# Moving the loads of the lanes earlier in a hybrid layer: the weight join, the rows of W1, the gains of W2 and W3, and the kept gate and up products

## The chip, the core and the metric

The kernel runs on one core of a Trainium2 chip. The core has five engines with a queue each: TensorE (PE) multiplies, VectorE (DVE) does elementwise arithmetic, ScalarE (ACT) does activations and copies, GpSimd (POOL) helps with elementwise work, and SyncE (SP) issues most of the transfers (DMA). ACT and POOL issue some transfers too. An engine runs its list strictly in the order in which the compiler left it, and an instruction that waits holds up all that stand behind it on its engine. Engines wait for each other by semaphores.

The metric is device time in microseconds for one execution, less is better. The kernel before took 2001.74 us (median of three runs, 1999.65 to 2007.75).

## The reference

One decoder layer over 2048 tokens of width 1024, all in fp32:

```python
hn = rms_norm(h, mix_pre_g)
proj = hn @ w_in
q = proj[..., :D_Q].reshape(B, S, N_Q_HEADS, HEAD_DIM)
k, v = ...                                   # 2 key heads
u = proj[..., D_Q + 2 * D_KV:]
attn_out = sliding_window_attention(q, k, v, attn_sinks, rel_bias)
conv_out = conformer_conv(u, conv_dw, conv_dw_b, conv_ln_g, conv_ln_b, w_conv_pw)
mixed = jnp.concatenate([attn_out, conv_out], axis=-1) @ w_out
h = h + rms_norm(mixed, mix_post_g)
hn = rms_norm(h, ffn_pre_g)
ff = (jax.nn.silu(hn @ w_gate) * (hn @ w_up)) @ w_down
h = h + rms_norm(ff, ffn_post_g)
```

The attention has a window of 128 tokens, 8 query heads on 2 key heads, a learned sink for each head and a relative bias. The convolution path is a gated unit, a causal depthwise convolution of 31 taps, a layer norm over the channels, a swish and a 512x512 product (`w_conv_pw`). The feed-forward width is 2816.

## The kernel before

**Products.** A product in fp32 is made from three products of a shorter format: each operand is split into a high part (ACT casts it: `split_w`, L133, and `split_f`, L811) and a low part (DVE or POOL subtracts: L135, L814), and PE adds high x high, high x low and low x high in PSUM (`three`, L188, `product`, L893). Rows and weights are split once and the halves kept (`lo_in`, `lo_out` hold the low halves of weights in DRAM).

**Stages.** The 2048 tokens go in four tiles of 512. A0 to A3 (`stage_a`) are the input projection of a tile, B0 to B3 (`stage_b`) its attention, T0 to T3 the taps of the convolution on DVE, C0 to C3 (`stage_tail`, `conv_tail`) its layer norm and swish. The results of B and C are written to `mixT` in DRAM, eight chunks of 128 channels. W0 to W3 (`stage_w`, L714) read a tile of `mixT` back, multiply it with the output projection and apply the norm and the residual (`norm_w`, L761), writing `h_scr` and `hn_scr`. J (`stage_join`, L621) multiplies `w_conv_pw` with the lower half of `w_out` once, so that W can use the product `w_join`. H makes the operands of the feed-forward from `hn_scr`: `stage_h_plain` (L843) loads a chunk, transposes it on PE, copies it with its gain into a `gb` tile (`u`, L849), writes that to `hT` in DRAM and splits it (L852); `stage_h_sums` (L856) makes sums of these.

The feed-forward works on two tiles of tokens at a time, as a block scheme with seven products for eight blocks. F0 and F2 are gate and up for the first and second pair. `stage_pre` (L901) makes two passes over the first 20 (F0) or 16 (F2) weight pairs: pass one multiplies with operand B11, copies the sum out of PSUM and writes it to `keeps` in DRAM; pass two (q at or over PRE) fetches it back into a `gb` tile (`fetch`, L919), ACT copies it into a PSUM bank (`seed`, L934, the copy on L938), and the product with B21 is added. `stage_p1` (L971) then goes through all weight pairs with the other five or seven products of each; where the product was kept, it fetches the kept sum once more (`fetch`, L1013) and ACT copies it into a bank (L1046). G0 and G2 (`stage_p2`, L1132) multiply with `w_down`, and the ends of G0 and G2 apply the last norm.

**Lanes.** The A, W1, F and G stages are run one after the other (`run`). Beside them stand lanes (class `Lane`, L1289): generators whose `yield` says how much PE time (in us) the step is taken to be worth; after each step of the main stage a lane gets credit at its rate and goes on as far as the credit reaches. The number behind a `yield` thus sets how much main work lies between two steps in the order of the program. J, C0 and C1 are one lane (`ld`), W0 and later C2, W2, C3, W3 another (`lw`), H a third (`lh`).

**Order.** The program is then scheduled by a list scheduler, which sets the order on each engine by its own estimates; the order of the program is its priority. So the order on the chip isn't that of the code, but it is fixed when the program is built.

**Buffers.** Tiles come from pools with a fixed number of buffers for each tag (`BUFS`, L53): two for `gb`, `at` and `mb`, one for `wx`, four for `fa` and `mid`. A new tile of a tag waits until an older one of it has been used. `gb` holds the gains of the norms (`load_gb`, L701), H's copies, the kept sums and one partial sum of `stage_p1`. `at` holds the rows of W1, W2 and W3 (L732), attention results of B on their way to `mixT`, and the rows of x in the norm (L786).

Of the kernel before, what the change touches and what calls it, by code (L numbers as in the profile page):

```python
# [25 lines left out]
P = 128  # L26
T = 512
NT = S // T
KC = D // P
# [8 lines left out]
def layer_kernel(ctx, tc, x, xT, cols, rows, sinks, relb, onehot, w_in, w_pw, w_out, w_gate, w_up, w_down, out):  # L38
    nc = tc.nc
# [21 lines left out]
    def f2(tag, shape=(P, T)):  # L61
        return t_(tag, shape)
# [558 lines left out]
    def stage_join():  # L621
        lab[0] = "J0"
        right = []
        for k in range(4):
            raw = f4("wx", (P, 2, T))
            nc.sync.dma_start(raw, w_out[4 + k].rearrange("p (a b) -> p a b", a=2))
            yield 1.5
            for n in range(2):
                lab[0] = "J0"
                right.append(split_w(raw[:, n], "mid" if k < 2 else "chl"))  # L630
            yield 1.5
            lab[0] = "J0"
        for mp in range(2):
            pair_ = t_("yt", (P, 2, 2, T), F32R)
            raw = f4("wx", (P, 2, T))
            nc.sync.dma_start(raw, w_pw[2 * mp : 2 * mp + 2].rearrange("m p t -> p m t"))
            yield 1.5
            lab[0] = "J0"
            left = [split_w(raw[:, m], pair_[:, m]).rearrange("p a (k c) -> p a k c", c=P) for m in range(2)]
            yield 2  # L640
            for m in range(2):
                for n in range(2):
                    lab[0] = "J0"
                    o = ct()
                    three(o, [((left[m][:, 0, k], left[m][:, 1, k]), (right[2 * k + n][:, 0], right[2 * k + n][:, 1])) for k in range(4)])
                    z = f2("fa")
                    act(z, o, AF.Copy, scale=0.5)
                    nc.scalar.dma_start(w_join[2 * mp + m, :, n * T : (n + 1) * T], z)
                    yield 4
                    lab[0] = "J0"  # L650
# [63 lines left out]
    def stage_w(w, spill, G, atag, htag, mtag, bank_of, norm=None):  # L714
        L = f"W{w}"
        lab[0] = L
        acc = [f4(atag) for _ in range(4)]

        def acts(gi, ms=None):
            aa = []  # L720
            for m in ms or load(gi):
                a = hl(htag)
                act(a[:, 0], m, AF.Copy)  # L723
                vtt(a[:, 1], m, a[:, 0].bitcast(F32), ALU.subtract)
                aa.append([a])
            return aa

        def load(gi):
            ms = []
            for c in range(G * gi, G * gi + G):  # L730
                ms.append(f2(mtag))
                nc.sync.dma_start(ms[-1], mixT[c, :, w * T : (w + 1) * T])  # L732
            return ms

        first = load(0)
        if w != 1:
            yield 5.0
            lab[0] = L
        nxt = acts(0, first)
        for gi in range(KC // G):  # L740
            aa = nxt
            for n in range(2):
                lab[0] = L
                if n == 0 and w != 1 and gi + 1 < KC // G:
                    rows_next = load(gi + 1)
                if n == 1 and gi + 1 < KC // G:
                    if w == 1 and G * gi + G == 4:
                        ld.until("C1")
                        lab[0] = L
                    nxt = acts(gi + 1, rows_next if w != 1 else None)  # L750
                src = w_out[2 * gi : 2 * gi + 2] if gi < 2 else w_join[2 * gi - 4 : 2 * gi - 2]
                ws = weight(src[:, :, n * T : (n + 1) * T].rearrange("c p t -> p c t"),
                            lo_out[n, 2 * gi : 2 * gi + 2], w > 0)
                yield from block_half(acc, list(zip(aa, ws)), n, gi == 0, L, bank_of)
        tail = norm_w(w, spill, acc, mtag)
        if norm:
            norm(tail)
        else:
            yield from tail

    def norm_w(w, spill, acc, mtag):  # L761
        L = f"W{w}"
        lab[0] = L
        gb = load_gb(0)
        ssq = sm(4)
        for s in range(4):
            act(junk, acc[s], AF.Square, accum_out=ssq[:, s : s + 1])
            yield 0.5
            lab[0] = L
        r = rsqrt(ssq, 4, D, w < 3)  # L770
        yield 3
        lab[0] = L
        ssq2 = sm(4)
        for s in range(4):
            lab[0] = L
            post_scale(acc[s], gb, r[:, s : s + 1])
            r0 = w * T + s * P
            if s == (2 if mtag == "fa" else 0):
                xt = f4("wx")
                nc.sync.dma_start(xt, x[r0 : r0 + P])  # L780
                vtt(acc[s], xt, acc[s], ALU.add)
            else:
                for n in range(2):
                    cs = slice(n * T, (n + 1) * T)
                    xt = f2(mtag if s == 1 or w > 1 else "fa")
                    nc.sync.dma_start(xt, x[r0 : r0 + P, cs])  # L786
                    vtt(acc[s][:, cs], xt, acc[s][:, cs], ALU.add)
            nc.sync.dma_start(h_scr[r0 : r0 + P], acc[s])
            act(junk, acc[s], AF.Square, accum_out=ssq2[:, s : s + 1])
            yield 5.0  # L790
        lab[0] = L
        r2 = rsqrt(ssq2, 4, D, w < 3)
        yield 3
        lab[0] = L
        for s in range(4):
            act(acc[s], acc[s], AF.Copy, scale=r2[:, s : s + 1])
            if spill:
                r0 = w * T + s * P
                nc.scalar.dma_start(hn_scr[r0 : r0 + P], acc[s])
        yield 0.1  # L800
        hns[w] = acc
# [99 lines left out]
    def stage_pre(ws, ops, mid, keep, q0=0, q1=None):  # L901
        PRE = PRES[ws[0]]
        q1 = q1 or 2 * PRE
        L = f"F{ws[0]}"
        raws = {}
        wops = {}
        kept = {}

        def load(q):
            if q < q1 and q % 2 == 0:  # L910
                lab[0] = L
                half, m = divmod(q, PRE)
                raw = t_("raw", (P, 2, T))
                for j in range(2):
                    src, pr = MATS[m + j]
                    nc.sync.dma_start(raw[:, j], src[2 * pr][:, half * T : (half + 1) * T])
                    raws[q + j] = raw[:, j]

        def fetch(q):  # L919
            if PRE <= q < q1:  # L920
                lab[0] = L
                kept[q] = f2("gb")
                nc.sync.dma_start(kept[q], keep[q - PRE])  # L923

        def split(q):
            if q < q1:
                lab[0] = L
                raw = raws.pop(q)
                wops[q] = split_f(raw, hl("w"))
                lo(raw, wops[q], ws[0] and q % 2 == 1)  # L930

        seeded = {}

        def seed(q):  # L934
            if PRE <= q < q1:
                lab[0] = L
                seeded[q] = mm()
                act(seeded[q], kept.pop(q), AF.Copy)  # L938

        load(q0)  # L940
        load(q0 + 2)
        for q in range(q0, q0 + 3):
            split(q)
        for q in range(q0, q1):
            half, m = divmod(q, PRE)
            started.add(f"P{ws[0]}.{q}")
            bn = "B21" if half else "B11"
            if len(ops.get(bn, ())) < 4:
                lh.until(f"{bn}.{ws[0]}")
            split(q + 3)  # L950
            load(q + 4)
            fetch(q + 2)
            lab[0] = L
            seed(q + 1)
            lab[0] = L
            o = seeded.pop(q) if half else mm()
            product(o, wops.pop(q), ops[bn], not half)
            if not half:
                u = f2("fa")
                act(u, o, AF.Copy)  # L960
                nc.scalar.dma_start(keep[m], u)
            else:
                if MATS[m][0] is w_gate:
                    sg = f2("fa")
                    act(sg, o, AF.Silu)
                else:
                    vtt(sg, sg, o, ALU.mult)
                    nc.sync.dma_start(mid[0, MATS[m][1]], sg)
            yield 2.76

    def stage_p1(ws, ops, mid, keep):  # L971
        PRE = PRES[ws[0]]
# [48 lines left out]
        for q in range(AHEAD):  # L1021
            split(q)
        loads(1)
        fetch(0)
        sg = {}
        for q, (m, j, i, nst) in enumerate(todo):
            pre = m < PRE
# [55 lines left out]
                        defer(2, lambda a=mid[6, pr], s=s: tied(nc.sync.dma_start(a, s)))  # L1083
            if j == nst - 4:
                sums(m + 1)
            if j == nst - 2:
                fetch(m + 1)
            if j == nst - 1:
                loads(m + 2)
# [262 lines left out]
    PRE_S0, PRE_S2 = 22, 16  # L1352
    H1, H2, H3, H4 = 0, 4, 7, 11
    NH = 24
    lb = Lane(RB, 0)
    lc = Lane(RC0, LC)
    lw = Lane(RW0, 0)
# [161 lines left out]
```

## Time and profile before

| | |
|---|---|
| median of three runs | 2001.74 us (1999.65 to 2007.75) |
| the profiled execution | 1996.83 us, its span 1994.7 us |
| mean granted TensorE clock | 0.991 |
| PE busy | 1939.1 us (97%) |
| DVE busy | 1490.7 us (75%) |
| ACT busy | 971.3 us (49%) |
| POOL busy | 332.6 us (17%) |
| moved by DMA | 452.49 MB, 227 GB/s in the mean |

In the profile an instruction is named by its line, engine, operation and tiles (`out<-in`, buffer numbers left out, the letter behind @ is the stage). `PE mm@W <- ACT hl@W` in a list of waits means that PE, about to multiply into a bank of W, stood idle until ACT had made a tile `hl` of W. Idle time of ACT or DVE costs nothing by itself; only what PE waits for does. The granted clock is the share of its full clock at which PE was allowed to run.

### The profile page before, as it was taken

The page shows a single profiled execution, that of the slowest core. Times are in us where ns is not written, and L with a number is a line of the kernel's source. Part 1 is how long each engine was busy: PE and PEld are TensorE (multiplying, and loading weights), DVE is VectorE, ACT ScalarE, POOL GpSimd, SP SyncE. Part 2 cuts the span into 40 slices and gives each one's busy share as a digit, 9 for nine tenths or more (in the row PEclk, how much of TensorE's full clock was granted, in tenths as well). Part 3 has the DMA queues.
Part 4 walks back from the last instruction along what each step waited for, and adds up shares of the span by engine and source line. Part 5 has one row for each costly group of instructions (what it writes and reads, how often), then busy time and mean ns, then how long its engine had stood idle before and what let it go on. Part 6 is the DMA issues. An engine that isn't in the chain of part 4 may idle for free. (4 is left out here: it accounts for less than half of the span.)

```text
span 1994.7 us, 26920 instructions
## 1 busy us (share of the span) xinstructions
PE 1939.1 (97%) x8730; PEld 1544.5 (77%) x8730; DVE 1490.7 (75%) x2679; ACT 971.3 (49%) x1910; POOL 332.6 (17%) x395
## 2 busy tenths in 40 slices
PE   8999999999899999999999999989999999999998
PEld 7877677677667878878878878778788888888886
DVE  5998997887684899988759985675866665545557
ACT  5355344646566733334355446656644333345443
POOL 5001312241110300000000020002523332311000
PEclk9999999999899999999999999999999999999999
DMA  8886656558759876787477677779844442366654
GB/s 309 266 308 212 205 160 199 183 187 283 247 187 330 288 255 227 238 279 261 157 265 249 228 266 267 234 275 349 310 143 169 169 153 101 125 223 212 210 182 162
DMA packets 234077, 452.49 MB, mean 227 GB/s; under 512 B 23464, under 2 KB 49232, under 8 KB 233936
## 3 DMA queue, kind: packets, MB, share of 16 engines
q1 hardware_dynamic: 212304, 415.11, 61.9%
q10 hardware_dynamic: 19392, 28.32, 3.9%
q0 software_dynamic: 2240, 7.34, 0.9%
q8 instruction: 69, 1.13, 0.2%
q14 instruction: 72, 0.59, 0.1%
HBM read 329.55 MB, written 121.12 MB: 226 GB/s over the span
## 5 line engine op out<-in xcount | busy, mean ns | idle before, releaser
L85 DVE SCALAR_TENSOR_TENSOR fc@C<-glu@C,colt,fc@C 128x512 f32<-128x512 f32 x480 | 369.2, 784 | 2.8
L108 PE MATMUL mm@F<-hl@H,w@F 128*128 128x512 f32 x1056 | 254.7, 391 | 0.0
L108 PE MATMUL mm@G<-hl@G,hl@G 128*128 128x512 f32 x924 | 225.2, 395 | 8.6 <-DVE x@G L85 6.0
L108 PEld LDWEIGHTS mm@F<-hl@H,w@F 128*128 128x128 f32 x1056 | 197.8, 188 | 41.5
L108 PE MATMUL mm@A<-hl@A,w@A 128*128 128x512 f32 x840 | 207.5, 396 | 3.9 <-ACT hl@A L319 1.4
L108 PEld LDWEIGHTS mm@G<-hl@G,hl@G 128*128 128x128 f32 x924 | 172.9, 189 | 47.8 <-ACT gb@H L849 6.2
L811 ACT ACTIVATE w@F<-chl@F 128x512 fp32r<-128x512 f32 x220 | 135.8, 625 | 136.9 <-PE mm@F L108 130.2
L108 PE MATMUL mm@G<-w@G,hl@G 128*128 128x512 f32 x876 | 199.5, 389 | 0.0
L108 PEld LDWEIGHTS mm@G<-w@G,hl@G 128*128 128x128 f32 x876 | 164.4, 188 | 34.2
L108 PEld LDWEIGHTS mm@A<-hl@A,w@A 128*128 128x128 f32 x840 | 155.8, 188 | 43.7 <-issue 4.2
L85 DVE TENSOR_TENSOR w@F<-chl@F,w@F 128x512 fp32r<-128x512 f32 x198 | 144.5, 731 | 39.4 <-ACT w@F L811 39.0
L108 PE MATMUL mm@F<-mid@H,w@F 128*128 128x512 f32 x528 | 133.2, 397 | 3.9 <-ACT mm@F L938 3.9
L108 PE MATMUL mm@F<-ql@H,w@F 128*128 128x512 f32 x528 | 128.2, 391 | 4.6 <-ACT w@F L811 4.6
L108 PE MATMUL mm@F<-p@H,w@F 128*128 128x512 f32 x528 | 130.3, 392 | 0.2 <-ACT at@F L1060 0.2
L108 PE MATMUL mm@F<-x@H,w@F 128*128 128x512 f32 x528 | 125.1, 390 | 0.0
L108 PEld LDWEIGHTS mm@F<-mid@H,w@F 128*128 128x128 f32 x528 | 99.5, 190 | 26.1 <-ACT mm@F L938 5.0
L108 PEld LDWEIGHTS mm@F<-ql@H,w@F 128*128 128x128 f32 x528 | 99.1, 188 | 25.9 <-ACT w@F L811 5.5
L108 PEld LDWEIGHTS mm@F<-p@H,w@F 128*128 128x128 f32 x528 | 99.9, 190 | 21.7 <-ACT at@F L1060 0.8
L108 PEld LDWEIGHTS mm@F<-x@H,w@F 128*128 128x128 f32 x528 | 98.8, 188 | 22.8 <-issue 2.4
L108 PE MATMUL mm@W<-w@W,hl@W 128*128 128x512 f32 x384 | 107.2, 413 | 4.9 <-ACT hl@W L723 3.6
L108 PE MATMUL tr@W<-w@W,ql@W 128*128 128x512 f32 x384 | 98.7, 397 | 4.3 <-ACT ql@W L723 3.4
L133 ACT ACTIVATE w@A<-raw@A 128x512 fp32r<-128x512 f32 x110 | 66.9, 626 | 73.3 <-PE mm@A L108 40.1
(301 smaller groups left out, 3274.7 us busy)
## 6 DMA issues: line engine op xcount, KB each, us to landing
mids<-fa@F SPq DMA_DIRECT2D x154, 256.0 KB, 2.8
raw@A<-w_in SPq DMA_DIRECT2D x55, 512.0 KB, 4.7
w@A<-lo_in SPq DMA_DIRECT2D x84, 256.0 KB, 3.8
fc@G<-mids SPq DMA_DIRECT2D x77, 256.0 KB, 3.4
fa@G<-mids SPq DMA_DIRECT2D x75, 256.0 KB, 4.6
gb@F<-keeps SPq DMA_DIRECT2D x72, 256.0 KB, 4.3
w@W<-lo_out SPq DMA_DIRECT2D x48, 256.0 KB, 4.3
raw@F<-w_gate SPq DMA_DIRECT2D x22, 512.0 KB, 3.4
```

Of the source, the lines that this page charges most:

```text
L85: r = op(*args, **kw)
L108: r = nc.tensor.matmul(*args, **kw)
L133: act(w[:, 0], raw, AF.Copy)
L811: act(w[:, 0], x, AF.Copy)
```

## The change

Four edits.

- J: between its loads and the splits that use them, the generator yields 10 (`JL`) instead of 1.5, for the four loads of `w_out` and the two of `w_pw`.
- W1: the rows from `mixT` go into one `mb` tile of two halves instead of two `at` tiles, and the rows of the next two chunks are loaded at the first half of a step (n == 0), as W0, W2 and W3 already do, instead of at the second (n == 1).
- W2 and W3: the gains are loaded at the start of the stage, ahead of its first products, instead of at the start of the norm; the first yield is 8.0 instead of 5.0.
- Kept sums: in `stage_pre`, `fetch(q + 3)` stands after `seed(q + 1)`, where `fetch(q + 2)` stood before it; at q + 2 == PRE keep 0 is fetched at both places. The first fetch of `stage_p1` is moved to the end of `stage_pre` (`early`), and its fetch of the next keep from step nst - 2 to step 1 of a weight pair.

```diff
@@ stage_join @@
             nc.sync.dma_start(raw, w_out[4 + k].rearrange("p (a b) -> p a b", a=2))
-            yield 1.5
+            yield JL
...
             nc.sync.dma_start(raw, w_pw[2 * mp : 2 * mp + 2].rearrange("m p t -> p m t"))
-            yield 1.5
+            yield JL
@@ stage_w @@
+        stage = t_("mb", (P, 2, T)) if w == 1 else None
+
         def load(gi):
             ms = []
             for c in range(G * gi, G * gi + G):
-                ms.append(f2(mtag))
+                ms.append(stage[:, c % 2] if w == 1 else f2(mtag))
                 nc.sync.dma_start(ms[-1], mixT[c, :, w * T : (w + 1) * T])
             return ms
 
         first = load(0)
+        gb = load_gb(0) if w > 1 else None
         if w != 1:
-            yield 5.0
+            yield 5.0 if w == 0 else 8.0
...
-                if n == 0 and w != 1 and gi + 1 < KC // G:
-                    rows_next = load(gi + 1)
-                if n == 1 and gi + 1 < KC // G:
+                if n == 0 and gi + 1 < KC // G:
                     if w == 1 and G * gi + G == 4:
                         ld.until("C1")
                         lab[0] = L
-                    nxt = acts(gi + 1, rows_next if w != 1 else None)
+                    rows_next = load(gi + 1)
+                if n == 1 and gi + 1 < KC // G:
+                    nxt = acts(gi + 1, rows_next)
...
-        gb = load_gb(0)
+        gb = gb or load_gb(0)
@@ stage_pre @@
-            if PRE <= q < q1:
+            if PRE <= q <= q1:
                 lab[0] = L
                 kept[q] = f2("gb")
-                nc.sync.dma_start(kept[q], keep[q - PRE])
+                nc.sync.dma_start(kept[q], keep[q - PRE if q < q1 else 0])
...
-            fetch(q + 2)
+            if q + 2 == PRE:
+                fetch(q + 2)
             lab[0] = L
             seed(q + 1)
+            fetch(q + 3)
...
+        early[ws[0]] = kept.pop(q1)
@@ stage_p1 @@
-        fetch(0)
+        kept[0] = early.pop(ws[0])
...
-            if j == nst - 2:
+            if j == 1:
                 fetch(m + 1)
@@ constants @@
+    JL = 10
```

More of the change, by code (lines that the diff above doesn't have):

```diff
@@ L754, in stage_w @@
                 yield from block_half(acc, list(zip(aa, ws)), n, gi == 0, L, bank_of)
-        tail = norm_w(w, spill, acc, mtag)
+        tail = norm_w(w, spill, acc, mtag, gb)
         if norm:
@@ L759, in stage_w, with norm_w @@
             yield from tail
-    def norm_w(w, spill, acc, mtag):
+    def norm_w(w, spill, acc, mtag, gb):
         L = f"W{w}"
         lab[0] = L
-        gb = load_gb(0)
+        gb = gb or load_gb(0)
         ssq = sm(4)
@@ L969, in stage_pre @@
             yield 2.76
+        early[ws[0]] = kept.pop(q1)
+    early = {}
     def stage_p1(ws, ops, mid, keep):
```

## The prediction

> **What bounds the kernel now.** I read the busy table first, then what TensorE (PE) waited for, then the granted clock around the long waits, then who held up the engine it waited for. The busy table, the core's clock and the waits of PE, longest sums first (total us, times, longest us):
>
> ```profile
> PE 1939.1 (97%) x8730; PEld 1544.5 (77%) x8730; DVE 1490.7 (75%) x2679; ACT 971.3 (49%) x1910; POOL 332.6 (17%) x395
> ...
> core 0: 1994.7 us, clock 0.991
> ...
> PE mm@G L108 <- DVE x@G L85: 6.0, 1, 6.0
> PE tr@B L108 <- DVE sm@B L460: 4.8, 2, 3.6
> PE mm@F L108 <- ACT w@F L811: 4.6, 2, 3.2
> PE mm@F L108 <- ACT mm@F L938: 3.9, 3, 1.9
> PE mm@W L108 <- ACT hl@W L723: 3.6, 2, 2.5
> PE tr@W L108 <- ACT ql@W L723: 3.4, 2, 3.2
> PE tr@B L108 <- ACT p@B L502: 3.3, 1, 3.3
> ...
> PE mm@W L108 <- DVE mid@W L85: 1.2, 1, 1.2
> ...
> PE tr@B L501 <- ACT gb@H L849: 1.0, 1, 1.0
> ```
>
> PE is the bound: 1994.7 - 1939.1 = 55.6 us of the span it is not busy, and the change leaves its instructions as they are (the instruction lists of the two built programs agree in number on every engine but SP, 1,339 to 1,341; a position below counts PE's instructions in such a list). So only idle PE time and slow-clock PE time can be won. The clock's 0.991 puts the second at about (1 - 0.991) x 1994.7 = 18 us. Where that lies is seen in the stretches after waits (columns: PE, weight load, DVE, ACT, POOL busy us and counts, granted clock, DMA share, GB/s):
>
> ```profile
> 529.50:532.80 3.30, 0.05 (x1) 0.00 (x0) 0.86 (x3) 3.30 (x18) 0.00 (x0) 0.90 0.52 156
> 532.80:538.40 5.60, 5.45 (x20) 1.95 (x21) 5.24 (x16) 0.57 (x2) 0.81 (x1) 0.50 0.42 140
> ...
> 547.00:551.00 4.00, 3.33 (x12) 2.10 (x12) 1.98 (x5) 4.00 (x17) 0.00 (x0) 1.00 0.40 107
> ...
> 736.90:740.10 3.20, 3.18 (x8) 2.50 (x9) 3.20 (x7) 1.49 (x3) 0.00 (x0) 0.51 0.83 267
> ...
> 1307.50:1313.50 6.00, 0.00 (x0) 0.01 (x1) 6.00 (x10) 3.70 (x7) 0.00 (x0) 0.74 0.72 213
> 1313.50:1317.10 3.60, 3.58 (x9) 2.83 (x10) 3.47 (x6) 0.10 (x2) 0.00 (x0) 0.50 0.95 348
> ```
>
> A wait of 2.5 us (up to 547.0) leaves the clock at 1.00; waits of 3.2, 3.3 and 6.0 us are followed by 3.2, 5.6 and 3.6 us at half clock, so each costs about 1.6, 2.8 and 1.8 us more than itself. The profiled run took 1996.83 us, 1994.7 us of it span; the median of the three timed runs is 2001.74, 4.9 us above. I make the sum on the profiled run and subtract it from the median.
>
> **The change part by part.**
>
> *First rows of W1 (staged in `mb`, asked for at n == 0).* Before, the rows are loaded into the two `at` buffers, which attention block B3 also uses. What ACT did there (start us, length us, engine, line, operation, tiles, in brackets the idle time before):
>
> ```profile
> 529.04 0.39 ACT L479 ACTIVATE p@B<-p@B,sm@B 128x128 f32<-128x128 f32 x1
> ...
> 532.22 0.57 ACT L502 ACTIVATE p@B<-tr@B 128x512 f32<-128x512 f32 x1
> ...
> 541.19 0.33 ACTq L850 DMA_DIRECT2D hT<-gb@H  x1
> ...
> 546.35 0.63 ACT L723 ACTIVATE hl@W<-at@W 128x512 fp32r<-128x512 f32 x1 [2.99 <-DMA at@W<-mixT]
> ```
>
> ACT's waits over the whole run, and of the transfers two that matter below (KB, median us to landing):
>
> ```profile
> ACT mm@F L1046 <- DMA gb@F<-keeps: 75.6, 28, 6.9
> ...
> ACT ql@W L723 <- DMA at@W<-mixT: 22.3, 8, 5.5
> ...
> ACT mm@F L938 <- DMA gb@F<-keeps: 18.0, 13, 3.5
> ...
> ACT hl@W L723 <- DMA at@W<-mixT: 16.7, 6, 4.7
> ...
> hT<-gb@H ACTq DMA_DIRECT2D x16, 256.0 KB, 3.8
> ...
> at@W<-x SPq DMA_DIRECT2D x14, 256.0 KB, 5.8
> ```
>
> The two waits of PE on `hl@W` (3.6) are rows that come late. In the old list the last four blocks of rows are asked for 12 to 17 matmuls before their first product, in the new one 170 or more; `at` no longer couples them to B3. I take 3.6 away. At 20 us for 90 matmuls (row below) 170 are 38 us of cover, against waits that were 4.7 us at most; late next are the low halves on DVE, made from the same rows.
>
> Because W1's rows are ready, the scheduler writes another order for 529 to 554 us. Before, ACT ran eight exponentials (529.04 to 532.2) ahead of the eviction `p@B` that PE was waiting for: that is the 3.3 us and its half-clock 2.8. In the new list that eviction (PE position 2362) stands ahead of the exponentials (2384), with twelve W1 matmuls (2.7 us) between the transposes and the product. The waits on `gb@H` (1.0) and on `mid@W` (1.2) sit in the same knot and go with it. Together 3.6 + 3.3 + 2.8 + 1.0 + 1.2 = 11.9 us, bounds 3.6 (only the rows) and 11.9.
>
> *The price: F0's start.* W1 now runs through undisturbed, and tr@H0#0 to #7 move behind it, from list positions 2366-2503 to 2458-2591, among the first four products of F0 (2486 on). Before, all H0 operands stood ready when F0 began. Costs of one, from 530 to 600 us, and the pace of PE:
>
> ```profile
> L811 ACT ACTIVATE w@F<-raw@F 128x512 fp32r<-128x512 f32 x12 | 7.5, 627 | 3.2 <-PE mm@W L108 3.1
> L849 ACT ACTIVATE gb@H<-tr@H,colt 128x512 f32<-128x512 f32 x8 | 5.4, 677 | 3.6 <-DVE x@H L85 1.8 <-PE tr@H L829 1.7
> L767 ACT ACTIVATE junk<-mid@W 128x1024 bf16<-128x1024 f32 x4 | 4.2, 1048 | 1.1 <-DVE mid@W L85 1.1
> L852 ACT ACTIVATE x@H<-gb@H 128x512 fp32r<-128x512 f32 x4 | 2.4, 621 | 0.4 <-ACT gb@H L849 0.4
> L528 ACT ACTIVATE at@B<-tr@B 128x512 f32<-128x512 f32 x3 | 1.8, 595 | 5.4 <-PE tr@B L108 5.4
> ...
> 1100.00:1120.00 20.00, 20.00 (x90) 16.57 (x89) 19.32 (x31) 5.88 (x10) 0.00 (x0) 1.00 0.76 256
> ```
>
> Between operand 0's cast and operand 1's, the new list gives ACT: two squares of `mid` (2.1), one `at` eviction (0.6), two `gb` copies (1.35), two weight casts (1.25), the cast itself (0.62): 5.9 us. PE has 12 products of 512 columns (0.22 each, 2.7) and 16 small transposes and scores, which I put at half a product or less (1.8): 4.5 us. So about 1.4 us late, once more of the kind behind operand 2, and DVE (which makes the low halves) in the same stretch has the taps besides. I take +3; bounds 0 and 10 (second rival).
>
> *Gains of W3 (and W2) fetched at the stage's start.* Before, W3's gain loads wait for two `gb` buffers held by H2's copies, DVE stands 3.26 us and then does eight post-scales, and the `x@G` copies PE needs at 1307.5 come out of the same queue 6.0 us late:
>
> ```profile
> 1300.83 2.74 DVE L85 SCALAR_TENSOR_TENSOR mid@W<-mid@W,sm@W,gb@W 128x512 f32<-128x512 f32 x4 [3.26 <-DMA gb@W<-rows]
> ...
> 1304.09 2.74 DVE L85 SCALAR_TENSOR_TENSOR mid@W<-mid@W,sm@W,gb@W 128x512 f32<-128x512 f32 x4
> ...
> 1312.68 1.89 DVE L85 TENSOR_TENSOR x@G<-x@G,mm@G 128x512 f32<-128x512 f32 x3
> ```
>
> In the new list the fetch is 590 PE positions earlier and the post-scales 30 positions earlier. But the gains now hold both `gb` buffers until the post-scales are done, so H2's first copies move back behind them, the w_down loads behind those on SP's queue (list position 5655 to 5682), and the next thing late is the x-row load `at@W<-x` (5.8 us), issued 20 positions before DVE needs it in front of the `x@G` copies. 20 positions are 4.4 us: about 1.4 us short by its median. The wait of 6.0 thus keeps something between 1.4 and nearly all; I take 4.0, still long enough for the half clock: -2. Bounds: -7.8 (6.0 and its 1.8 all gone), +1.
>
> W2's fetch (list position 4405 to 4403) and its row loads (4456 in both) were already placed there: the 3.2 us at `ql@W` stays, 0 (bounds -4.8 if it goes with its half clock, +0).
>
> *Keep fetches.* A keep needs one of the two `gb` buffers, and in both lists each fetch stands right behind the copy (L938) that frees one, or in the five-step stage behind the write of `mids` that SP was waiting for. Asking for it earlier in the program doesn't give it a buffer. The waits of 75.6 and 18.0 us on ACT stay, and with them PE's 4.6 and 3.9: 0 (bounds -10.1, both sums and the half clock behind 736.9; +1, for the two extra 256 KB fetches of keep 0, which nobody reads).
>
> *The join (JL = 10).* Its 96 products move from list position 971 to 1110, and C0's tail from 1388 to 1584, C1's end from 2045 to 2149. They are PE work either way, and C1's rows are still written a hundred matmuls or more before W1's products read them: 0 by themselves. The wait of 3.6 on `sm@B` lies at 223 us, where DVE's list is unchanged: it stays. But every engine's order from 223 to 600 us is dealt anew; I put +2 for new short waits (bounds -4 and +8).
>
> Sum: -11.9 + 3 - 2 + 0 + 0 + 2 = **-8.9 us**, 1987.9 for a profiled run, **1993** for the median.
>
> [...] The row of half clock behind a wait of 3.3 us is 532.8 to 538.4. [...]
>
> **The rivals.**
>
> *All named waits go.* Keeps, gains and W2's rows too: 11.9 + 7.8 + 4.8 + 10.1 = 34.6, less 5 for the new ones: 1972. Against it: two `gb` buffers, and lists that show the same gates. With the gain wait alone gone beside W1's it is -11.9 - 7.8 + 5 = -14.7, 1987.
>
> *H0 on two buffers (the other side).* The eight copies of H0 go through two `gb` buffers, each free only when its write to hT has landed. With 0.68 for the copy, 0.33 for the issue and 3.8 for hT, four rounds take 19.2 us, and PE's list there has 48 products and 60 small ones, about 17 us. At 5.8 (what `at@W<-x` takes) four rounds are 27.2: 10 us late, and three waits long enough for half clock, 1.6 each: 15. Then -11.9 + 15 - 2 + 2 = +3, 2005. It decides from an hT of about 5 us. For it: PE's first products alternate with the transposes in the list; against it: only operands 0 to 3 are needed by B11's products, the other four a pass later.
>
> *The change does little.* The order is dealt anew, and waits of the old size stand elsewhere: 0 +- 4, 2001. For it: two of four edits move nothing in the lists. Against: the 3.3 us eviction is plainly mended.
>
> **How the numbers follow.** Forecast (-4 to -14) 0.48; all of the rest or the gain wait goes too 0.12; does little 0.22; H0 on two buffers 0.18. A measurement here can tell about 0.5%, 10 us: faster is below 1991.7, slower above 2011.7. Faster: two fifths of the first (0.20), the second (0.12), a little of the third (0.02): 0.34. Slower: a third of the last (0.06), where its waits double, and 0.08 for new waits in the order dealt anew that no row shows. Range: 1982 (first case at its far end, with the gain wait gone) to 2009 (H0's waits, 4 above 2005); the likeliest case's own is 1988 to 1998.
>
> **What would show it.** Right: no wait of PE on ACT `p@B` L502 or `hl@W` between 500 and 560 us, granted clock 1.00 there; ACT's wait on keeps still near 75; `gb@W<-rows` gone from DVE's waits; a wait on `x@G` of 2 to 5 us left; small waits of `mm@F` on `x@H` or `gb@H` near 570. Wrong: a wait of over 3 us on `x@H`, `gb@H` or hT with half clock behind it, or waits in A2, A3 and W0 that sum to over 5 us more, or keep waits that shrink.

## The result, and the profile after

The changed kernel took 1990.45 us, median of 8 runs (1984.09 to 1997.53), beside 2001.24 us for the kernel before on the same chip: a ratio of 0.9945, 95% interval 0.9924 to 0.9967, or 11 us (7 to 15) less. The forecast was 1993, with a sum of -8.9 us.

The recorded run of the changed kernel was the slowest of its eight (1997.53 us, span 1995.6, clock 0.989) and that of the kernel before lay 4 us below its median, so the trace of the changed kernel is 1 us the longer although its median is 11 us less: the traces show at which places time was won and lost, the medians how much.

The waits of PE in the changed kernel (total us, times, longest):

```profile
PE mm@F L108 <- ACT mm@F L941: 11.5, 11, 2.8
PE mm@W L108 <- ACT hl@W L723: 5.6, 3, 3.9
PE tr@B L108 <- POOL p@B L504: 4.4, 1, 4.4
...
PE tr@W L108 <- ACT ql@W L723: 2.7, 1, 2.7
...
PE mm@W L108 <- ACT x@W L696: 1.9, 1, 1.9
...
PE mm@G L108 <- DVE x@G L85: 1.4, 1, 1.4
...
PE mm@F L108 <- DVE x@H L85: 0.9, 1, 0.9
```

The wait of 3.3 on `p@B` (L502), the late rows at 547 us, `mid@W` and `gb@H` are gone, and the 6.0 on `x@G` is 1.4. In their place stand a wait of 3.9 on `hl@W` and one of 1.9 on `x@W` (both in W0), and many small ones on the copies of kept sums (L941, which was L938). The 4.4 on `p@B` of POOL, at 217 us, takes the place of the 3.6 that stood on `sm@B` at 223 us before, and of smaller ones: from 200 to 300 us PE is idle for 4.4 us after 4.7. The busy time by stretches shows the exchange. Before (columns as in the prediction):

```profile
300.00:400.00 100.00, 98.75 (x460) 70.28 (x459) 82.76 (x184) 53.96 (x129) 25.60 (x35) 1.00 0.61 193
400.00:500.00 100.00, 99.40 (x450) 72.80 (x448) 80.24 (x148) 52.93 (x116) 28.57 (x47) 1.00 0.73 238
500.00:600.00 100.00, 90.75 (x441) 64.94 (x441) 74.30 (x193) 59.22 (x148) 15.40 (x32) 0.95 0.64 213
600.00:700.00 100.00, 100.00 (x454) 80.55 (x453) 63.38 (x92) 66.95 (x118) 20.05 (x24) 1.00 0.90 310
...
1300.00:1400.00 100.00, 93.98 (x420) 77.49 (x419) 69.10 (x139) 62.55 (x123) 19.02 (x35) 0.97 0.90 317
1400.00:1500.00 100.00, 96.10 (x426) 78.44 (x425) 73.33 (x91) 50.58 (x91) 36.05 (x24) 0.98 0.62 221
```

The changed kernel:

```profile
300.00:400.00 100.00, 94.25 (x441) 67.84 (x440) 94.36 (x205) 46.16 (x116) 22.14 (x22) 0.97 0.51 165
400.00:500.00 100.00, 98.33 (x458) 73.19 (x458) 56.96 (x117) 62.38 (x127) 26.91 (x58) 1.00 0.73 236
500.00:600.00 100.00, 99.04 (x471) 71.09 (x470) 83.20 (x211) 60.47 (x151) 13.86 (x30) 0.97 0.68 224
600.00:700.00 100.00, 94.67 (x428) 74.68 (x425) 63.95 (x91) 65.45 (x115) 22.29 (x26) 1.00 0.90 312
...
1300.00:1400.00 100.00, 98.45 (x441) 80.49 (x440) 66.39 (x135) 65.37 (x129) 24.00 (x36) 0.98 0.94 335
1400.00:1500.00 100.00, 91.94 (x407) 74.14 (x406) 71.06 (x91) 48.68 (x88) 35.49 (x23) 1.00 0.62 215
```

PE's idle time falls by 8.3 us from 500 to 600 (W1) and by 4.5 from 1300 to 1400 (G0 beside W3). It rises by 5.6 from 300 to 500 (W0), by 5.3 from 600 to 700 (F0) and by 4.2 from 1400 to 1500 (F2, where the waits on kept sums go from 3.9 to 7.3 us).

What happened in W0 is seen in the order of ACT in the changed kernel (start us, length us, engine, line, operation, tiles):

```profile
353.41 0.39 ACT L479 ACTIVATE p@B<-p@B,sm@B 128x128 f32<-128x128 f32 x1
...
356.11 0.39 ACT L479 ACTIVATE p@B<-p@B,sm@B 128x128 f32<-128x128 f32 x1
...
356.49 0.62 ACT L723 ACTIVATE hl@W<-fa@W 128x512 fp32r<-128x512 f32 x1
```

Eight exponentials, 3.1 us in a row, stand ahead of the cast `hl@W` that PE waits for; the row to be cast landed at 353.77, just after the first of them began. It is the same arrangement as the one before the 3.3 us wait at 529 us in the kernel before, at another place and ahead of another instruction. Its price beside the wait is half clock, here one stretch (the granted clock is the third number from the end):

```profile
357.20:361.20 4.00, 4.00 (x10) 3.13 (x11) 3.96 (x11) 1.05 (x3) 0.00 (x0) 0.50 0.82 302
```

### The profile page after: what moved, and what is told of

The parts are those of the page before. It is cut to its first block, busy times and chain, and to the rows that moved or that the text cites. A ratio compares the mean times of both kernels' runs of the same rounds, so it can differ in the third digit from the quotient of the medians.

```text
span 1995.6 us, 26899 instructions
## 1 busy us (share of the span) xinstructions
PE 1940.2 (97%) x8730; PEld 1546.2 (77%) x8730; DVE 1488.0 (75%) x2679; ACT 970.8 (49%) x1910; POOL 331.1 (17%) x395
## 4 chain that ended last, share of the span: by engine, by line
PE 76%; DMA 9%; DVE 8%; issue 3%; ACT 3%; POOL 1%; SPq 0%; ACTq 0%; DVEq 0%; POOLq 0%
PE mm@F L108 30%; PE mm@G L108 18%; PE mm@A L108 14%; PE mm@W L108 4%; PE tr@W L108 4%; PE tr@B L108 3%; DMA gb@F<-keeps 2%; DVE fc@C L85 1%; PE ct@J L108 1%; DVE mid@W L85 1%; DMA mixT<-fc@C 1%; DVE w@F L85 1%; DMA chl@F<-w_up 1%; DVE fa@F L85 1%; DVE chl@F L85 1%
## 5 line engine op out<-in xcount | busy, mean ns | idle before, releaser
L85 DVE TENSOR_TENSOR w@G<-raw@G,w@G 128x512 fp32r<-128x512 f32 x73 | 51.2, 701 | 67.6 <-ACT w@G L814 66.6
```

The costliest lines, as they stand in the source:

```text
L85: r = op(*args, **kw)
```

## The experiments

The changed kernel was run again, and then each part alone and the whole without one part. A ratio is that to the kernel before, with its 95% interval.

| kernel | median us | ratio | interval |
|---|---|---|---|
| changed, again | 1988.66 | 0.9940 | 0.9917 to 0.9964 |
| W1's rows alone | 1997.98 | 0.9970 | 0.9954 to 0.9986 |
| gains alone | 1996.52 | 0.9963 | 0.9945 to 0.9982 |
| kept sums alone | 1999.13 | 0.9991 | 0.9975 to 1.0007 |
| join alone | 2005.32 | 1.0012 | 0.9998 to 1.0026 |
| all but the join | 1992.51 | 0.9954 | 0.9936 to 0.9972 |
| all but W1's rows | 1997.00 | 0.9982 | 0.9964 to 1.0000 |
| all but the kept sums | 1993.41 | 0.9961 | 0.9942 to 0.9979 |
| before, exponentials later | 1994.62 | 0.9965 | 0.9949 to 0.9980 |
| before, kept sums not fetched | 1984.18 | 0.9910 | 0.9889 to 0.9930 |
| before, W3's gains early, yield 5.0 | 2001.84 | 1.0006 | 0.9990 to 1.0022 |
| all but the join, exponentials later | 1989.39 | 0.9935 | 0.9911 to 0.9958 |

**The changed kernel again** (no edit).

> The changed kernel once more, for a second profile: the profiled run on record, 1997.5 us, is the slowest of its eight, so one profile may show waits that are the run's and not the kernel's. Theory: the ratio to before stays at 0.993 to 0.996; the waits that the order on the engines sets come back at the same places (3.9 us on ACT hl@W near 357 us, 4.4 on POOL p@B near 217), and those on kept sums (11.5 us on ACT mm@F L941) come back with other sizes, 4 to 12 us. Rival: the 11.5 us come back within 2 us, so they belong to the kernel.

0.9940 repeats 0.9945. The waits that the order sets come back: 3.9 us on `hl@W` in W0, and 4.7 us near 227 us, now on `sm@B` instead of POOL's `p@B`. Those on kept sums come back as 8.9 us after 11.5, which is what the theory allowed and a little too far off for the rival.

**W1's rows alone.**

```diff
+        stage = t_("mb", (P, 2, T)) if w == 1 else None
...
-                ms.append(f2(mtag))
+                ms.append(stage[:, c % 2] if w == 1 else f2(mtag))
...
-                if n == 0 and w != 1 and gi + 1 < KC // G:
+                if n == 0 and gi + 1 < KC // G:
```

> Only the rows of W1 staged in mb and asked for at n == 0. Theory: 11.9 us of waits and half clock between 529 and 568 us go, about 3 us come back at F0's start: -9 us, ratio 0.9955 (0.993 to 0.998), and no wait of PE on ACT p@B L502 or hl@W between 500 and 570 us. Rival (the gain of the whole came from other waits that the new order happens to lack): within 3 us of before.

-6 us (-9 to -3). The wait on `p@B` and those on late rows are gone, but ACT has the eight exponentials ahead of H0's copies instead (this kernel, order on ACT):

```profile
548.24 0.39 ACT L479 ACTIVATE p@B<-p@B,sm@B 128x128 f32<-128x128 f32 x1
...
551.03 0.39 ACT L479 ACTIVATE p@B<-p@B,sm@B 128x128 f32<-128x128 f32 x1
...
551.93 0.67 ACT L851 ACTIVATE gb@H<-tr@H,colt 128x512 f32<-128x512 f32 x1
```

and PE's waits between 500 and 580 us have this row at their head:

```profile
PE tr@H L831 <- ACT gb@H L851: 4.3, 2, 3.5
```

The knot has moved 20 us on. In the changed kernel, with the join's other order, H0 is dealt behind W1 and this wait isn't there.

**The gains alone.**

```diff
+        gb = load_gb(0) if w > 1 else None
         if w != 1:
-            yield 5.0
+            yield 5.0 if w == 0 else 8.0
...
-        gb = load_gb(0)
+        gb = gb or load_gb(0)
```

> Only the gains of W2 and W3 fetched at the stage's start, with the yield of 8. Theory: the wait of 6.0 us on x@G and its 1.8 us of half clock shrink, nothing else moves: -2 to -7 us, ratio 0.9965 to 0.999; W2's wait of 3.2 us on ql@W stays. Rival: the buffers held longer put a new wait of about 3 us into W3 or H2 and eat the gain: 0 +- 2 us.

-7 us (-11 to -4): by its median the largest of the four parts, and just past the far end of what the theory gave. `x@G` keeps a wait of 0.9, and the clock around it stays full (this kernel), where the prediction's rows show 0.74 and 0.50 at that place before:

```profile
1300.00:1320.00 20.00, 18.97 (x81) 14.78 (x80) 16.45 (x27) 12.77 (x24) 0.00 (x0) 1.00 1.03 374
```

**The kept sums alone.**

```diff
-            fetch(q + 2)
+            if q + 2 == PRE:
+                fetch(q + 2)
             lab[0] = L
             seed(q + 1)
+            fetch(q + 3)
...
-            if j == nst - 2:
+            if j == 1:
                 fetch(m + 1)
```

> Only the kept sums fetched earlier. Theory: two gb buffers gate the fetches in both versions: 0 +- 2 us, PE's waits on ACT mm@F L941 or L938 stay within 3 us of before's 3.9, and ACT's wait at the second fetch near 75 us. Rival: the fetch that stands behind the seed comes later than before and the waits of pass two grow to 8 to 12 us in all: +4 to +8 us, ratio 1.002 to 1.004.

No difference that can be told from none, as the theory said. ACT's waits on them (this kernel) shrink:

```profile
ACT mm@F L1051 <- DMA gb@F<-keeps: 70.8, 29, 4.5
...
ACT mm@F L938 <- DMA gb@F<-keeps: 12.6, 12, 2.1
```

from 75.6 and 18.0, but PE's wait on the copies is 3.4 after 3.9, and the wait on `w@F` behind them 4.3 after 4.6. ACT's idle time was mostly not on PE's path.

**The join alone.**

```diff
-            yield 1.5
+            yield JL
...
+    JL = 10
```

> Only the join's yields of 10. The three other edits alone measured 0.9970 (W1's rows), 0.9963 (gains) and 0.9991 (keeps), together -15 us, the whole 0.994, -12. Theory (the edits add): the join costs about +3 us, ratio 1.0015 (1.000 to 1.003), from waits at W0's start near 357 us (3.9 on ACT hl@W with half clock behind it) and near 217 to 228 us (4.4 to 4.7). Rival (the edits don't add, the join is harmless and the others overlap): 0.999 to 1.0005, and no wait of 3.9 us near 357.

+2.4 us, with zero just inside the interval. The waits of PE show where (this kernel):

```profile
PE mm@W L108 <- ACT hl@W L723: 13.0, 5, 4.0
...
PE tr@B L108 <- ACT p@B L502: 0.7, 1, 0.7
```

The 3.9 us at W0's start are one of the five. Two others, 3.3 and 4.0 us, lie in W1. The join's order alone thus undoes the knot at `p@B` (3.3 to 0.7) and ties others: the first of the two in W1 again has eight exponentials ahead of it on ACT (534.4 to 537.6 us), the second waits for a row that landed late, at 541.0 us.

**The whole without one part.** The edits are those above, turned round.

Without the join:

```diff
-            yield JL
+            yield 1.5
```

> The whole change without the join's edit. Theory (the edits add): -15 us, ratio 0.9925 (0.991 to 0.994), better than the whole by about 3; PE reaches its last product of A near 496 us instead of 501 to 503, and pass two of F0 (600 to 700 us) has no idle PE, as in the three single edits. Rival (the waits of 5 us in 600 to 700 belong to W1's rows and the keeps together): they stay, and the ratio is 0.994 or above.

0.9954, outside what the theory gave (0.991 to 0.994): leaving the join out of the whole gains nothing. Of its signs two hold, the last product of A begins at 494 us and PE is not idle from 600 to 700 us. What is back is the wait of W1 alone, 3.5 us on `gb@H` at 550 us.

Without W1's rows:

```diff
-                ms.append(stage[:, c % 2] if w == 1 else f2(mtag))
+                ms.append(f2(mtag))
...
-                if n == 0 and gi + 1 < KC // G:
+                if n == 0 and w != 1 and gi + 1 < KC // G:
```

> The whole change without W1's rows. Theory (the edits add): -6 us, ratio 0.997 (0.995 to 0.9985), and the wait of 3.3 us on ACT p@B L502 and those on hl@W are back between 520 and 570 us. Rival (the join's new order is enough to undo the knot at 530 us): ratio 0.9935 to 0.995, no wait on p@B there.

0.9982, as the theory gave, but not by the wait that it named. On `p@B` only 0.7 us stand here, as the rival said, since the join's order has undone that knot; what is back from 500 to 600 us are waits on `hl@W` (this kernel):

```profile
PE mm@W L108 <- ACT hl@W L723: 6.1, 2, 3.3
```

Without the kept sums' edit:

```diff
+            fetch(q + 2)
...
-            fetch(q + 3)
...
-            if j == 1:
+            if j == nst - 2:
```

> The whole change without the keeps' edit. Theory (it does next to nothing): ratio 0.994 to 0.996, and the waits of the whole on kept sums in pass two of F0 (3 to 5 us in 600 to 700 us) are there too, since they come from an earlier F0. Rival (the fetch behind the seed makes them): 600 to 700 us without idle PE, ratio 0.992 or below.

0.9961, at the edge of the theory. 3.0 us of waits on kept sums stand from 600 to 700 us, so they are not made by this edit.

Taken out of the whole, W1's rows are worth 0.0037 (7 us), the kept sums 0.0016 (3 us) and the join 0.0009 (2 us, a gain here, a loss alone); the last two lie within the intervals. The four parts alone sum to -6.0 - 7.4 - 1.8 + 2.4 = -12.8 us beside -11 measured. The whole without the gains' edit was not run.

**The exponentials later, in the kernel before.** They get a later place in the scheduler's list, and nothing else is touched:

```diff
+            late = tc.cur_priority
+            tc.cur_priority = late + 150
             for h in range(8):
                 act(pr[:, h], pr[:, h], AF.Exp, bias=negm[:, h : h + 1], accum_out=den[:, h : h + 1])
+            tc.cur_priority = late
```

> The kernel before with one thing changed: the eight exponentials of a block in B are given a lower priority in the scheduler's list (150 steps later), so that the eviction p@B (L502) that PE waits for at 529.5 us stands ahead of them on ACT. W1's rows are as before, nothing is left out. Theory (the block of eight exponentials, 3.1 us of ACT, ahead of work that PE needs is the cause of that wait; late rows are a separate one): the 3.3 us wait and its 2.8 us of half clock go, the hl@W waits of about 3.6 us stay: -5 to -6 us, ratio about 0.997, provided that the wait does not come back at gb@H near 550 us as it did in W1 alone. Rival (the rows cause both): the eviction is late in any order, the 3.3 us stay in some form between 525 and 560 us, ratio 1.000 within 0.001.

-7 us (-10 to -4). The eviction (L505 here) now stands ahead of the exponentials:

```profile
529.38 0.58 ACT L505 ACTIVATE p@B<-tr@B 128x512 f32<-128x512 f32 x1
529.86 0.39 ACT L481 ACTIVATE p@B<-p@B,sm@B 128x128 f32<-128x128 f32 x1
```

and of PE's waits from 500 to 580 us these are the largest and the one in question:

```profile
PE mm@W L108 <- ACT hl@W L726: 2.2, 3, 1.0
...
PE tr@B L108 <- ACT p@B L505: 0.8, 1, 0.8
```

So a change of order on ACT, with the loads of W1's rows left as they were in the program, is worth as much as W1's edit. The 3.3 us shrink to 0.8 and the half clock behind them goes (0.76 from 526 to 540 us before, 1.00 here), as the theory said. The edit deals the order anew for every block of B, and in the recorded run what is won by the start of F0 (4.0 us) is lost again in F0; where the 7 us of the median lie is not shown. Nor does it follow that earlier rows are worth little: under the join's order W1's edit is worth 7 us, with the 6.1 us on `hl@W` shown above.

**The kept sums not fetched, in the kernel before.**

```diff
-                act(seeded[q], kept.pop(q), AF.Copy)
+                act(seeded[q].rearrange("p (a b) -> p a b", b=P), ident.unsqueeze(1).to_broadcast([P, 4, P]), AF.Copy)
```

(the same on L1046, and the fetches taken out).

> The kernel before, without fetching the kept sums at all: the copy into the PSUM bank (L938 and L1046) reads a constant tile that is always there, so the second halves of the kept products are not added (left out: the kept sums and their 60-odd transfers back; everything else is there). This bounds from above what any earlier fetch of the kept sums can bring. Theory (PE's waits on keep copies are 3.9 in pass two and one of 4.6 near 736 us sits in the same place, with half clock behind it): at most about -8 to -10 us, ratio 0.995 to 0.996, and the part of the change that touches fetches (measured -1.8 alone) gets a fifth of it. Rival (ACT's waits of 75.6 and 18.0 are covered by PE's queue of products): -4 us or less, ratio 0.998 to 1.000.

-18 us (-22 to -14), nearly twice the 10 that the prediction gave as the most that could be won. The waits of 4.6 on `w@F` and of 3.9 on the copies are gone; of PE's waits in F0 from 580 to 1010 us one row is left:

```profile
PE mm@F L108 <- DVE gb@F L85: 0.9, 1, 0.9
```

The change got a tenth of what lies there at most. In the recorded runs F0 and F2 together, from the first product of each to the first of the G behind it, take 13.2 us less than before; 8.1 of these are idle time of PE and 3.4 half clock. So at most some 2 us can be a faster pace of the products. Whether the waits go because nothing waits for kept sums or because other loads land sooner (72 fetches of 256 KB are 18.9 MB less) was not separated.

**W3's gains alone, with the yield at 5.0.**

```diff
+        gb = load_gb(0) if w > 2 else None
...
-        gb = load_gb(0)
+        gb = gb or load_gb(0)
```

> The kernel before with only W3's gains loaded at the start of the stage; W2's stay late, and the first yield stays 5.0 in all stages. Theory (the gain's part comes from W3's post-scales that no longer stand 3.26 us on DVE in front of the x@G copies): the same as both gains with the yield of 8.0, -7 us, ratio about 0.9965, x@G wait 1 to 2 us near 1310. Rival (the first yield of 8.0 places the loads sooner and does part of it): -2 to -4 us, ratio about 0.9985, with the x@G wait still at 4 us or more.

Neither theory held: the wait on `x@G` went, and the time did not. PE's waits in this kernel:

```profile
PE mm@F L108 <- ACT mm@F L939: 6.2, 6, 1.7
...
PE ct@C L559 <- DMA fc@C<-y_scr: 2.2, 1, 2.2
PE mm@G L108 <- DVE x@G L85: 1.6, 1, 1.6
```

With W3's gains alone 2.2 us of waiting (1.6 in the kernel before) end at 1172 us on a load of C's rows, and 2.3 us more than before stand on the kept sums of F2; with both gains and the yield the first is not there. The recorded runs are 2 and 7 us shorter in span than the one before. So removing the named wait is not enough; W2's early gains or the larger yield, or the order that comes with them, carry the rest. Which of these was not tried.

**All but the join, exponentials later** (both edits above).

> The changed kernel without the join's longer yields, and with the exponentials of B at the lower priority (150 steps). In the changed kernel without the join alone (ratio 0.9954) a wait of 3.5 us stood near 550 us, again behind eight exponentials that held up gb@H and x@H on ACT. Here six of the eight still stand ahead of the second x@H, and the eviction p@B (L502) stands second among them instead of behind all. Theory (that block is what is left of the knot): the wait near 550 us shrinks from 3.5 to about 2.4 us and loses its half clock, -2 to -4 us more: ratio 0.9935 to 0.9945. Rival (the order of ACT there does not matter, PE waits for the transposes' banks): 3.5 us stay, ratio 0.9954 within 0.001.

0.9935, inside what the theory said. The wait near 550 us is 2.9 instead of 3.5, now on `p@B`, but half clock still follows it (last section); that part of the theory fails. Beside 0.9954 without the later exponentials, and 0.9945 and 0.9940 for the changed kernel, the intervals overlap: it isn't shown to be a better version.

## Why the prediction was right, and where it was not

**W1's rows, -11.9.** Measured alone the edit brings F0's start with it, so the term to compare is -11.9 + 3 = -8.9: -6.0 alone, -7 out of the whole. It was 2 to 3 us too large, within the interval. The reason for the 3.3 us (eight exponentials on ACT ahead of an eviction) was right, and is shown by the later exponentials. What failed is the step "and go with it": alone, the block of exponentials stops H0's copies 20 us later. In the changed kernel all of it does go (9.2 us idle from 500 to 600 us become 1.0), but the order that allows this comes from the join, which has its own price in W0. And the clock there is not 1.00, as the prediction said it would be if right: 6.8 us of half clock stand from 509.7 us, with no wait ahead of them (last section).

**F0's start, +3.** The wait foreseen on `x@H` is 0.9, and hT lands in 3.8 us, far from the 5 from which two buffers would have decided. Instead 4.3 us of small waits on kept sums stand from 600 to 700 us, in a stretch that was full before. They are not there without the join or without W1's rows, so they come with the order that these two make together. H0's copies are now inside F0 and use the same two `gb` buffers, but the last of them is done at 594 us and the first of these waits ends at 646; what makes the waits stays open.

**The gains, -2.** Undersized: alone -7.4. The forecast that 4 of the 6.0 us would stay, for the x rows, fails. The order on DVE in the changed kernel:

```profile
1291.53 5.39 DVE L85 SCALAR_TENSOR_TENSOR mid@W<-mid@W,sm@W,gb@W 128x512 f32<-128x512 f32 x8
...
1306.28 1.35 DVE L85 TENSOR_TENSOR mid@W<-at@W,mid@W 128x512 f32<-128x512 f32 x2 [2.80 <-DMA at@W<-x]
...
1308.75 1.88 DVE L85 TENSOR_TENSOR x@G<-x@G,mm@G 128x512 f32<-128x512 f32 x3
```

The x rows are late indeed, by 2.8 us, but the post-scales end 10 us sooner, and PE sees 1.4 of it. Half clock follows even so in this trace, where it stayed away with the gains alone:

```profile
1308.41:1311.82 3.41, 1.86 (x6) 0.97 (x6) 3.41 (x7) 3.41 (x8) 0.00 (x0) 1.00 1.03 385
1311.82:1315.23 3.41, 3.41 (x9) 2.62 (x8) 3.41 (x7) 1.89 (x4) 0.00 (x0) 0.50 1.04 401
```

The wait by itself does not account for the 7 us either: W3's gains alone take it from 6.0 to 1.6 and bring no time. W2's gains and the yield were put at 0, and that run shows that at least one of them matters. DVE's wait on `gb@W<-rows` is gone in W3, as foreseen; one of 2.9 us now stands at 601 us, in W1.

**W2, 0.** The wait on `ql@W` at 1027 us stays, 2.7 after 3.2, as said.

**The kept sums, 0.** Right in size: 0.9991 alone. ACT's waits on them (changed kernel):

```profile
ACT mm@F L1054 <- DMA gb@F<-keeps: 93.5, 30, 7.7
...
ACT mm@F L941 <- DMA gb@F<-keeps: 21.4, 15, 4.0
```

They grew where 75 was foreseen, and alone they shrank a little (70.8). The two `gb` buffers as the gate were not tested. Without any fetch it is -18, beyond the bound of -10.1; an earlier fetch need not reach that.

**The join and the order, +2.** Alone +2.4, and at a place the prediction named: waits in A3 and W0 grow by 5.6 us of idle time and half clock behind them. That meets one of its conditions for being wrong, a sum over 5 us. It was outweighed by the gains, which came out 5 us better.

**The sum.** -8.9 against -11 is nearer than its terms: W1 with F0's start was taken 2 to 3 us too high, the gains 5 and the kept sums 2 too low. That these partly cancel is luck. The chance that it would be faster by over 0.5% was put at 0.34 and within 0.5% at 0.52; -0.55% lies just over the line, whose two sides the interval spans.

**The clock behind a wait.** I went by the traces, that 2.5 us leave the clock and 3.2 take it. The runs show no such line: 1.4 us on `x@G` were followed by half clock (above), 2.9 us at 1260 us were not. What the traces show around two waits of the same length is in the last section.

## What to carry to other kernels

When an in-order engine gets a block of many small instructions (here 3.1 us of exponentials), look for what PE needs from it next, and try one priority before moving any transfer: that alone gave as much as the edit of W1's rows. Sum a change by parts that are each run alone, since a moved load also deals the order of every engine anew, and the knot it unties can be tied again a little further on. Before tuning a fetch, run the kernel with the fetched tile always present: it bounds what there is to win, and shows that long waits on ACT may hide a small wait of PE (here 75.6 and 18.0 us on kept sums, beside PE's 3.9 on the copies and 4.6 behind them). Don't price the half clock behind a wait by the length of the wait alone: here one wait of 2.93 us was followed by half clock and another of 2.93 us by full clock, each in its own kernel (next section).

## What was not expected of the hardware

A wait took the clock or not in a way that its length alone does not tell. In the traces of the kernel before and of the changed one the granted clock is 0.50 in stretches of 3.41 us (five in each) and 6.83 us (two before, three in the changed kernel), apart from one behind the last product; and in each of the two traces these stretches begin whole multiples of 3.413 us apart (before at 228.36, 504.84, 532.14 us and so on, in the changed kernel at 31.82, 216.14, 356.09 us and so on). The rows below are divided at the same distance. In the kernel with all but the join and the exponentials later, a wait of 2.93 us (545.03 to 547.96) lies inside one row, in which PE was busy for 0.48 us, and the next row is at half clock:

```profile
544.94:548.35 3.41, 0.48 (x3) 0.20 (x4) 0.69 (x1) 3.41 (x14) 0.46 (x2) 1.00 0.94 272
548.35:551.76 3.41, 3.41 (x12) 1.01 (x8) 3.05 (x7) 2.04 (x5) 0.26 (x1) 0.50 0.61 199
```

In the changed kernel a wait of the same 2.93 us (1259.47 to 1262.40) is divided between two rows, in which PE was busy for 2.29 and 1.61 us, and the clock stays full:

```profile
1257.20:1260.62 3.42, 2.29 (x11) 1.55 (x9) 0.27 (x1) 0.93 (x2) 0.00 (x0) 1.00 0.94 252
1260.62:1264.03 3.41, 1.61 (x7) 1.35 (x8) 3.41 (x7) 2.30 (x5) 0.00 (x0) 1.00 1.04 327
1264.03:1267.44 3.41, 3.41 (x17) 2.83 (x16) 3.38 (x7) 2.17 (x5) 0.00 (x0) 1.00 0.89 312
```

In the traces of before and of the changed kernel, in the last 3.41 us ahead of each stretch of half clock (but for the place that comes next, and the end), PE was busy for 0.21 to 1.48 us in the kernel before and for 0.05 to 1.86 us in the changed one. In the changed kernel 1.61 us (the second row above) and 1.74 us (1417.63 to 1421.04) were followed by full clock all the same. So no one amount of idle time at which the clock falls is shown.

And there is half clock with no wait ahead of it. In the changed kernel, and then in its second run:

```profile
506.28:509.69 3.41, 3.41 (x12) 1.73 (x11) 1.14 (x2) 1.04 (x2) 2.35 (x8) 1.00 1.01 363
509.69:516.51 6.82, 6.82 (x16) 4.94 (x16) 5.93 (x16) 4.90 (x6) 0.00 (x0) 0.50 0.93 311
```

```profile
510.11:520.35 10.24, 10.24 (x21) 6.46 (x21) 5.93 (x16) 5.64 (x7) 1.15 (x6) 0.50 0.85 293
```

PE is never idle there (busy for 6.82 of 6.82 us, and for 10.24 of 10.24), and yet the clock is 0.50. The kernel before has 3.41 us of it at this place (504.84 to 508.25 us), the kernel without the edit of the kept sums none (1.00 from 504 to 520 us). In this stretch single score products stand between single products of W, 0.74 us for a pair at full clock (second run, order on PE):

```profile
506.94 0.49 PE L108 MATMUL mm@W<-w@W,hl@W 128*128 128x512 f32 x1
507.37 0.38 PE L108 MATMUL tr@B<-kz,ql@A 64*128 64x256 f32 x1
507.68 0.49 PE L108 MATMUL mm@W<-w@W,hl@W 128*128 128x512 f32 x1
...
522.08 0.97 PE L108 MATMUL tr@B<-kz,ql@A 64*128 64x256 f32 x12
```

Twelve such score products in a row take 0.97 us, 0.08 each, and a product of 512 columns in a row of its like takes 0.22 (the prediction's row), so the work of a pair would take 0.30. By this estimate PE is busy there but does less than half the work. That this takes the clock was the author's guess; no run tried it. The stretch of half clock begins 0.4 us later in the second recorded run of the changed kernel than in the first, counted from each run's first instruction, and is 3.41 us longer. Counted at half its length, which is an estimate, that makes these two runs differ by 1.7 us at this one place (half of 10.24 less 6.83).
